# Stick-breaking attention: the two heads of a pair in one step, logits on the halves of the array's rows, values on the halves of its columns with the operands exchanged

## The chip, the cores and the metric

One core of a Trainium2 chip runs the whole program; seven others lie idle. The metric is the device time of one execution in microseconds (us). TensorE (PE in the profile) multiplies matrices, VectorE (DVE) and ScalarE (ACT) work element by element, GpSimd (POOL) starts the gathers, SyncE (SP) starts the other transfers.

## The reference, cut to what matters

One decoder layer on 1024 tokens of width 1024: a mixer of three branches (stick-breaking attention, sparse attention, HGRN2 recurrence), and then PEER, a layer of 16384 small experts of which each token takes 128. The change touches the first branch alone, which has 8 heads of 64:

```python
for i in range(T // Q_BLOCK):                      # blocks of 128 queries
    q0 = i * Q_BLOCK
    kl = q0 + Q_BLOCK
    z = jnp.einsum("bhtd,bhsd->bhts", q[:, :, q0:kl], k[:, :, :kl]).astype(jnp.float32) * scale
    before = jnp.arange(kl)[None, :] < (q0 + jnp.arange(Q_BLOCK))[:, None]
    log_1m = jnp.where(before, jax.nn.log_sigmoid(-z), 0.0)
    after = lax.cumsum(log_1m, axis=3, reverse=True) - log_1m
    a = jnp.where(before, jnp.exp(jax.nn.log_sigmoid(z) + after), 0.0)
    outs.append(jnp.einsum("bhts,bhsd->bhtd", a.astype(v.dtype), v[:, :, :kl]))
```

So block i of queries needs i + 1 blocks of 128 keys: 36 blocks for a head, 288 for the eight.

## The kernel before

**Stages.** The tokens go through the mixer in four parts of 256. A part has four rounds; each round takes one head of HGRN2 (`hg`), one group and token tile of the sparse attention (`ns`) and one pair of heads of the stick-breaking attention (`sb`). The experts of parts 1 and 2 are then computed for all tokens by TensorE ("dense": 128 blocks of 48 matmuls, L1353 on). Parts 0 and 3 have theirs fetched row by row: 1024 gathers of 512 KB (L1104, L1114), each followed by one VectorE instruction of 1024 columns (L1106, L1116). 420 of these rows are paced to go beside the mixer, the others beside the dense experts. The mixer ends, and the dense products of the second kind begin, at about 2071 us.

**Items and pieces.** The branches' chains are lists of items of up to four stages. In step t of the order of emission the first stage of item t goes out, then the second of t-1, the fourth of t-3, the third of t-2 (L1302). What stands on its own (projections, merges, norms, scores, routes, the spreading of the gates) is cut into pieces. Each step is filled with pieces up to an even load:

```python
RPE, RDVE, REND, PD = 3.5, 3.0, 5.0, 1.2           # L24: work of TensorE and VectorE that a step is filled up to
for p in todo:                                     # L1297: pieces whose latest step has come go first
    if p.before > t:
        break
    p.emit(t)
```

A piece has a latest step; where it is reached the piece goes out whatever the load is (here called forced). The rows are paced by step numbers too: none before step 135, then 420 in proportion to the steps' TensorE work (L26, L1075). A scheduler then orders each engine's queue from this; what it made can be read in the built program, engine by engine.

**The branch that is changed** (`sb_items`, L372). An item is one head, one tile of 128 queries and up to 512 keys. `logits` (L381): one fp32 matmul of 64 rows (the head's width) into a PSUM bank `z`, for the first keys the mask as a second matmul (L387), then Abs, Relu, Exp, Ln on ScalarE. `weights` (L394): a running sum on VectorE (L397), its last column kept for the next chunk, a subtraction that reads `z` again (L401) and frees it, an Exp. `turned` (L404): transposes by TensorE into a bank `tr`, a copy `aT` to SBUF. `values` (L411): for each block of 128 keys a matmul with `aT` (128 columns) as the stationary operand and 64 columns of `v` moving; the result has the queries on the partitions. At the end of a round `out` and `out2` (L426, L430) copy the result, transpose it back by TensorE and split it into two float16 parts.

There are two banks `z` (ZB, L30), three banks `tr`, one bank `ov` and eight buffers `at` (e, r and aT of this branch, and what others keep for a short time). The heads of a pair lie on partitions 0 to 63 and 64 to 127 of `q` and `k`.

An fp32 matmul that is no transpose stands in the trace as two weight loads and two matmuls.

Of the kernel before, what the change touches and what calls it, by code (L numbers as in the profile page):

```python
# [36 lines left out]
# operands of the large products are split into two float16 parts after scaling by these powers of two  # L37
# [4 lines left out]
# scales of the gates, of their spread over the experts, and of the activations in the dense experts  # L42
# [5 lines left out]
# block numbers in the stream of projection weights  # L48
# [5 lines left out]
class Part:  # L54
    """a run of tokens that goes through the mixer together"""
# [8 lines left out]
# the parts whose tokens go through all experts; the others' experts are gathered  # L64
# [5 lines left out]
def trunk(ctx: ExitStack, tc: tile.TileContext, a: dict, out: bass.AP):  # L70
# [13 lines left out]
    # what the mixer alone needs  # L84
# [44 lines left out]
    # strictly causal block in reversed key order: key 127 - x, allowed where 127 - x < p  # L129
# [3 lines left out]
    # causal block: key x allowed where p - x >= 0  # L133
# [3 lines left out]
    # for each length of segments: keys of a first half before queries of the second, the second halves' queries only  # L137
# [7 lines left out]
    # distances to the keys of the window and to the ends of the blocks, negative; far under where the key isn't seen  # L145
# [11 lines left out]
    # lower bounds: cumulative softmax over the layers less the first layer's share  # L157
# [12 lines left out]
    # the window's keys and values: this part's and the one's before  # L170
# [49 lines left out]
    def load_w(blk, name, pt, br=False):  # L220
        """a block of weights in two parts; split for the first part, kept in DRAM for the others"""
# [29 lines left out]
    def transposed(src, name, pre=False):  # L251
        """the 128-column blocks of src transposed, side by side in one bank"""
# [44 lines left out]
    # Work comes in two kinds. Pieces stand on their own (projections, norms, merges); items are steps of the  # L297
    # branches' chains, each cut into four stages so that several can be under way at once.
# [37 lines left out]
    def sb_pieces(p, pt, st):  # L336
# [3 lines left out]
        def keep(t, d):  # L340
            # the tokens of earlier parts come back from DRAM
# [10 lines left out]
        # keys and values in reversed token order  # L352
# [19 lines left out]
    def sb_items(p, pt, st):  # L372
# [3 lines left out]
        def chunk(tl, hh, c0, c1, W):  # L376
            r0, n, b = T - W, c1 - c0, hh * 64
            un = f"{nm}_{tl}_{hh}_{c0}"
            x = {}

            def logits():  # L381
                z = ps_z.tile([128, 512], F32, tag="z", name=f"z_{un}")
                x["e"] = e = W2(f"e_{un}")
                x["z"], x["ee"] = z[:, 0:n], e[:, 0:n]
                P.matmul(x["z"], st["q"][b:b + 64, tl * 128:(tl + 1) * 128], st["k"][b:b + 64, r0 + c0:r0 + c1], start=True, stop=(c0 > 0))
                if c0 == 0:
                    P.matmul(z[:, 0:128], identb, sbmask, start=False, stop=True)  # L387
                x["r"] = W2(f"r_{un}")[:, 0:n]
                S.activation(x["ee"], x["z"], AF.Abs)
                S.activation(x["r"], x["z"], AF.Relu)  # L390
                S.activation(x["ee"], x["ee"], AF.Exp, scale=-1.0)
                S.activation(x["ee"], x["ee"], AF.Ln, bias=1.0)

            def weights():  # L394
                ee = x["ee"]
                # sum of softplus from the last key down, the key itself included
                V.tensor_tensor_scan(ee, x["r"], ee, 0.0 if c0 == 0 else st["prev"], op0=ALU.add, op1=ALU.add)  # L397
                if c1 < W:
                    st["prev"] = SM(f"prev_{un}", [128, 1])
                    V.tensor_copy(st["prev"], x["e"][:, n - 1:n])  # L400
                V.tensor_tensor(ee, x["z"], ee, op=ALU.subtract)  # L401
                S.activation(ee, ee, AF.Exp)

            def turned():  # L404
                tr = ps_tr.tile([128, TH], F32, tag="tr", name=f"tra_{un}")
                for c in range(0, n, 128):
                    P.transpose(tr[:, c:c + 128], x["e"][:, c:c + 128], ident)
                x["aT"] = W2(f"aT_{un}")
                S.activation(x["aT"][:, 0:n], tr[:, 0:n], AF.Copy)

            def values():  # L411
                if tl == 0 and hh == 0 and c0 == 0:
                    st["ov"] = ps_ov.tile([128, 4, 128], F32, tag="ov", name=f"ov_{nm}")
                for c in range(0, n, 128):
                    vb = r0 + c0 + c
                    P.matmul(st["ov"][:, tl, b:b + 64], x["aT"][:, c:c + 128], st["v"][:, vb + b:vb + b + 64], start=(c0 + c == 0), stop=(c0 + c == W - 128))
# [3 lines left out]
        for tl in range(pt.nt):  # L420
            W = 128 * (pt.ti0 + tl + 1)
            for hh in range(2):
                for c0 in range(0, W, 512):
                    res.append(chunk(tl, hh, c0, min(W, c0 + 512), W))

        def out():  # L426
            st["o"] = W2(f"o_{nm}", (128, pt.n))
            S.activation(st["o"], st["ov"][:, 0:pt.nt].rearrange("p a b -> p (a b)"), AF.Copy)

        def out2():  # L430
            oh, ol = branch_out(pt, 0)
            tr = transposed(st["o"], f"o_{nm}")
            split(oh[:, p, :], ol[:, p, :], tr, SO[0])

        res.append([None, None, out, out2])
        return res

# [1 line left out]
    def nsa_kv_pieces(pt, st):  # L439
# [22 lines left out]
        # compression of keys and values: block c takes the pieces c and c + 1 of 16 tokens.  # L462
        # Two neighbouring positions lie one under the other on the partitions; columns: position pair, group, block
# [3 lines left out]
        def pieces(which):  # L467
# [13 lines left out]
            # the last piece is kept for the next part  # L481
# [48 lines left out]
    def nsa_items(g, tl, pt, st, kv):  # L530
# [9 lines left out]
        # compressed branch  # L540
        def c_logits():
# [6 lines left out]
            # a column of nothing before the first block  # L548
# [19 lines left out]
        def c_select():  # L568
            # importance of the blocks: the heads' weights of the five pieces that overlap; sure blocks at the top
# [7 lines left out]
            # the four best are struck out, by value and place  # L577
# [6 lines left out]
        def c_rows():  # L584
            # the block bias and the distance penalty as further rows of the queries
# [18 lines left out]
        # the selection is found and used while the window's heads go on  # L604
        res = [[c_logits, c_norm, c_turn, c_values], [None, c_select, None, None], None, [None, None, c_rows, None]]

        # window branch, then selected branch, one head at a time
        sums = {}

        def head(br, i):  # L610
# [9 lines left out]
            def logits():  # L620
# [3 lines left out]
                # logits, negative, and the least of them  # L624
# [77 lines left out]
    def hg_pieces(h, pt, st):  # L702
        """projections of a head: values token-major; gates raw"""
# [21 lines left out]
    def hg_items(h, pt, st):  # L725
# [770 lines left out]
```

## Time and profile before

| | |
|---|---|
| three runs | 3733.98, 3744.84, 3757.71 us; median 3744.84 |
| span of the profiled execution | 3722.6 us; its own time with what lies around the span is not on the page |
| busy share of the span | PE 88%, PEld 59%, DVE 82%, ACT 42%, POOL 34% |
| mean TensorE clock granted | 0.921 |
| bytes moved | 1055.48 MB, mean 284 GB/s |

The three runs lie within 0.6% of each other. A window's row names a stretch of the span in us, and the busy time of each engine in it; a timeline's row gives the start, the time from the first start to the last end, and how many equal instructions follow each other. Matmuls are pipelined, so that the time of one is longer than the interval from its start to the next one's.

### The profile page before, as it was taken

Reading aid. Unit: us, or ns where it says so; the run is one execution under the profiler, and the core shown is the slowest. Engines: PE = TensorE matmul, PEld = TensorE weight load, DVE = VectorE, ACT = ScalarE, POOL = GpSimd, SP = SyncE. Lnnn points to the kernel's source line nnn. Section 1 sums busy time; section 2 is a strip of 40 time slices with the busy share of each in tenths; the row PEclk is TensorE's granted clock in tenths of the full one; section 3 lists DMA queues with packets and bytes.
Section 4 is the critical chain, followed back from the end, with each engine's and each line's share of the span. In section 5 each row is a group of like instructions: output and inputs, shape, how many; then the busy total and the mean of one; then the engine's idle time right before and its main releaser. Section 6 shows DMA issues by size and latency. Waiting matters only on the chain. (4 is left out here: it accounts for less than half of the span.)

```text
span 3722.6 us, 57637 instructions
## 1 busy us (share of the span) xinstructions
PE 3285.9 (88%) x20660; PEld 2191.0 (59%) x20660; DVE 3035.8 (82%) x7067; ACT 1572.2 (42%) x3110; POOL 1275.4 (34%) x1167
## 2 busy tenths in 40 slices
PE   6999999999986999898878897859999999999993
PEld 5887777777875777786566453424444444444441
DVE  5665689788799888789988678988888887888886
ACT  4776456554444564554457223323232223223222
POOL 0000002343322432233222344144555554555554
PEclk9999999999995999898577999979999999999996
DMA  7964857889974878877465999579999999999987
GB/s 260 334 243 144 295 189 274 317 308 325 328 273 147 300 256 300 296 278 261 142 208 195 356 332 325 193 273 339 333 337 325 320 337 322 346 332 318 334 287 261
DMA packets 359916, 1055.48 MB, mean 284 GB/s; under 512 B 35814, under 2 KB 108330, under 8 KB 355532
## 3 DMA queue, kind: packets, MB, share of 16 engines
q0 software_dynamic: 147456, 536.94, 41.5%
q1 hardware_dynamic: 212172, 514.86, 38.7%
q8 instruction: 162, 2.65, 0.3%
q14 instruction: 126, 1.03, 0.1%
HBM read 943.66 MB, written 108.00 MB: 283 GB/s over the span
## 5 line engine op out<-in xcount | busy, mean ns | idle before, releaser
L1114 POOL DMA_INDIRECT v<-in_peer_v_dram,gidx x512 | 655.1, 1280 | 872.7 <-DVE gacc L1116 590.8
L1104 POOL DMA_INDIRECT u<-in_peer_u_dram,gidx x512 | 605.9, 1183 | 869.1 <-DVE u L1106 599.4
L242 PE MATMUL g<-h,us 128*128 128x512 f16 x3072 | 712.5, 390 | 109.0 <-DVE acc L1383 71.4
L1116 DVE SCALAR_TENSOR_TENSOR gacc<-v,act,gacc 128x1024 f32<-128x1024 f32 x512 | 654.6, 1278 | 112.2 <-DMA v<-in_peer_v_dram,gidx 104.8
L1106 DVE SCALAR_TENSOR_TENSOR u<-u,gh 128x1024 f32<-128x1024 f32 x512 | 618.1, 1219 | 124.6 <-DMA u<-in_peer_u_dram,gidx 123.2
L242 PEld LDWEIGHTS <-us 128*128 128x128 f16 x3072 | 306.1, 100 | 497.8 <-issue 115.4
L1375 PE MATMUL acc<-vs,ac 128*128 128x512 f16 x2304 | 536.3, 384 | 33.1 <-ACT ac L200 28.4
L1375 PEld LDWEIGHTS <-ac 128*128 128x128 f16 x3072 | 302.9, 99 | 414.2 <-ACT ac L200 30.9
L242 PE MATMUL pj_mg<-hT,w_mg 128*128 128x256 f16 x2304 | 279.1, 277 | 16.3 <-ACT mg L859 9.5
L242 PEld LDWEIGHTS <-w_mg 128*128 128x128 f16 x2304 | 229.5, 101 | 48.8 <-issue 20.7
L200 ACT ACTIVATE vs<-vraw 128x1024 f16<-128x1024 f32 x128 | 133.8, 1048 | 270.3 <-DMA vraw<-in_peer_v_dram 270.1
L200 ACT ACTIVATE ac<-ge 128x512 f16<-128x512 f32 x128 | 79.9, 626 | 365.8 <-DVE ge L1368 250.0
L1335 ACT ACTIVATE ge<-g 128x512 f32<-128x512 f32 x128 | 75.6, 590 | 362.7 <-PE g L242 362.6
L1375 PE MATMUL g<-vs,ac 128*128 128x512 f16 x768 | 179.5, 385 | 9.6 <-DVE ts L958 7.3
L201 DVE SCALAR_TENSOR_TENSOR vs<-vraw,vs 128x1024 f16<-128x1024 f32 x128 | 155.2, 1217 | 23.2 <-ACT vs L200 23.2
L1174 PE MATMUL gb<-hot 128*128 128x128 f16 x512 | 126.3, 295 | 44.6 <-ACT stage L1177 28.9
L1177 ACT ACTIVATE stage<-gb 128x512 f32<-128x512 f32 x128 | 131.9, 1070 | 79.0 <-DMA d_G<-stage 45.2
L200 ACT ACTIVATE us<-uraw 128x1024 f16<-128x1024 f32 x128 | 134.0, 1049 | 68.2 <-DMA uraw<-in_peer_uT_dram 52.6
L242 PE MATMUL pb<-o,w_b 128*128 128x256 f16 x1152 | 141.6, 279 | 19.4 <-DMA w_b<-dw 9.3
L201 DVE SCALAR_TENSOR_TENSOR us<-uraw,us 128x1024 f16<-128x1024 f32 x128 | 155.7, 1218 | 2.9 <-ACT us L200 2.7
L242 PE MATMUL pj_r_hg<-hT,w_r_hg 128*128 128x256 f16 x1152 | 138.2, 277 | 1.5 <-ACT iv_hg L715 0.7
L242 PEld LDWEIGHTS <-w_b 128*128 128x128 f16 x1152 | 113.8, 101 | 42.6 <-issue 14.5
(1133 smaller groups left out, 5944.0 us busy)
## 6 DMA issues: line engine op xcount, KB each, us to landing
uraw<-in_peer_uT_dram SPq DMA_DIRECT2D x128, 512.0 KB, 6.7
vraw<-in_peer_v_dram SPq DMA_DIRECT2D x128, 512.0 KB, 6.2
w_mg<-dw SPq DMA_DIRECT2D x72, 512.0 KB, 6.3
d_G<-stage SPq DMA_DIRECT2D x32, 1024.0 KB, 5.1
gt<-d_G SPq DMA_DIRECT2D x32, 1024.0 KB, 13.2
w_r_hg<-dw SPq DMA_DIRECT2D x36, 512.0 KB, 5.7
w_b<-dw SPq DMA_DIRECT2D x72, 256.0 KB, 5.9
wr_mg<-in_wblk_dram SPq DMA_DIRECT2D x24, 512.0 KB, 5.1
```

What stands on the lines that cost most here:

```text
L200: S.activation(hi, src, AF.Copy, scale=scale)
L201: V.scalar_tensor_tensor(lo, in0=src, scalar=scale, in1=hi, op0=ALU.mult, op1=ALU.subtract)
L242: P.matmul(ps, l[:, k, :], r[:, k, :], start=(i == 0), stop=(i == n - 1))
L1104: G.indirect_dma_start(out=ur, out_offset=None, in_=a["peer_u"], in_offset=bass.IndirectOffsetOnAxis(ap=idx[:, c:c + 1], axis=0))
L1106: V.scalar_tensor_tensor(ur, in0=ur, scalar=1.0, in1=h2, op0=ALU.mult, op1=ALU.mult, accum_out=hpre[:, c:c + 1])
L1114: G.indirect_dma_start(out=vr, out_offset=None, in_=a["peer_v"], in_offset=bass.IndirectOffsetOnAxis(ap=idx[:, c:c + 1], axis=0))
L1116: V.scalar_tensor_tensor(acc, in0=vr, scalar=act[:, c:c + 1], in1=acc, op0=ALU.mult, op1=ALU.add)
L1174: P.matmul(ps[:, n, :], hs[:, 0, :, n], hs[:, 2, :, n], start=True, stop=False)
L1177: S.activation(stage[0][:, :, m0:m0 + 4].rearrange("p i n -> p n i"), ps, AF.Copy, scale=SA / SGT)
L1335: S.activation(ge, ps, AF.Gelu, scale=1.0 / (SW * SH2))
L1375: P.matmul(ps, ac[:, x, t * 128:(t + 1) * 128], v[:, y, dh * 512:(dh + 1) * 512], start=start and n == 0, stop=stop and n == 2)
```

## The change

An item is now a pair of heads: `logits` issues the two matmuls one behind the other, the first head's on rows 0 to 63 of the array into one bank `z`, the second's on rows 64 to 127 into the other, and then each head's mask and ScalarE work. `weights` and `turned` do one head after the other. `values` has `v` (64 columns) as the stationary operand and `aT` (128 columns) moving; the two heads alternate, the first on columns 0 to 63 of the array, the second on columns 64 to 127. The result has the channels on the partitions already, so the copy, the transposes back and one stage of the last item go. The items of a round fall from 5 to 3 in parts 0 and 1, from 9 to 5 in parts 2 and 3; 456 items become 408. The constants (RPE, PACE0 and so on) stay. Elsewhere comments alone are gone, so that line numbers behind this place are higher by 3.

```diff
-        def chunk(tl, hh, c0, c1, W):
-            r0, n, b = T - W, c1 - c0, hh * 64
-            un = f"{nm}_{tl}_{hh}_{c0}"
-            x = {}
+        def chunk(tl, c0, c1, W):
+            r0, n = T - W, c1 - c0
+            un = f"{nm}_{tl}_{c0}"
+            heads = [{}, {}]
             def logits():
-                z = ps_z.tile([128, 512], F32, tag="z", name=f"z_{un}")
-                x["e"] = e = W2(f"e_{un}")
-                x["z"], x["ee"] = z[:, 0:n], e[:, 0:n]
-                P.matmul(x["z"], st["q"][b:b + 64, ...], st["k"][b:b + 64, ...], start=True, stop=(c0 > 0))
-                if c0 == 0:
-                    P.matmul(z[:, 0:128], identb, sbmask, start=False, stop=True)
-                x["r"] = W2(f"r_{un}")[:, 0:n]
-                ...
+                for hh, x in enumerate(heads):
+                    b = hh * 64
+                    x["zt"] = z = ps_z.tile([128, 512], F32, tag="z", name=f"z_{un}_{hh}")
+                    x["z"] = z[:, 0:n]
+                    P.matmul(x["z"], st["q"][b:b + 64, ...], st["k"][b:b + 64, ...], start=True, stop=(c0 > 0))
+                for hh, x in enumerate(heads):
+                    if c0 == 0:
+                        P.matmul(x["zt"][:, 0:128], identb, sbmask, start=False, stop=True)
+                    ...
             def weights():
-                ...
+                for hh, x in enumerate(heads):
+                    ...
             def turned():
-                ...
+                for hh, x in enumerate(heads):
+                    ...
             def values():
-                if tl == 0 and hh == 0 and c0 == 0:
-                    st["ov"] = ps_ov.tile([128, 4, 128], F32, tag="ov", name=f"ov_{nm}")
+                if tl == 0 and c0 == 0:
+                    st["ov"] = ps_ov.tile([128, TH], F32, tag="ov", name=f"ov_{nm}")
                 for c in range(0, n, 128):
                     vb = r0 + c0 + c
-                    P.matmul(st["ov"][:, tl, b:b + 64], x["aT"][:, c:c + 128], st["v"][:, vb + b:vb + b + 64], ...)
+                    for hh, x in enumerate(heads):
+                        b = hh * 64
+                        P.matmul(st["ov"][b:b + 64, tl * 128:(tl + 1) * 128], st["v"][:, vb + b:vb + b + 64], x["aT"][:, c:c + 128], ...)
         for tl in range(pt.nt):
             W = 128 * (pt.ti0 + tl + 1)
-            for hh in range(2):
-                for c0 in range(0, W, 512):
-                    res.append(chunk(tl, hh, c0, min(W, c0 + 512), W))
+            for c0 in range(0, W, 512):
+                res.append(chunk(tl, c0, min(W, c0 + 512), W))
         def out():
-            st["o"] = W2(f"o_{nm}", (128, pt.n))
-            S.activation(st["o"], st["ov"][:, 0:pt.nt].rearrange("p a b -> p (a b)"), AF.Copy)
-        def out2():
             oh, ol = branch_out(pt, 0)
-            tr = transposed(st["o"], f"o_{nm}")
-            split(oh[:, p, :], ol[:, p, :], tr, SO[0])
-        res.append([None, None, out, out2])
+            split(oh[:, p, :], ol[:, p, :], st["ov"][:, 0:pt.n], SO[0])
+        res.append([None, None, None, out])
```

More of the change, by code (lines that the diff above doesn't have):

```diff
@@ new lines, in logits @@
+                for hh, x in enumerate(heads):
+                    b = hh * 64
+                    x["zt"] = z = ps_z.tile([128, 512], F32, tag="z", name=f"z_{un}_{hh}")
+                    x["z"] = z[:, 0:n]
+                    P.matmul(x["z"], st["q"][b:b + 64, tl * 128:(tl + 1) * 128], st["k"][b:b + 64, r0 + c0:r0 + c1], start=True, stop=(c0 > 0))
+                for hh, x in enumerate(heads):
+                    if c0 == 0:
+                        P.matmul(x["zt"][:, 0:128], identb, sbmask, start=False, stop=True)
+                    x["e"] = e = W2(f"e_{un}_{hh}")
+                    x["ee"] = e[:, 0:n]
+                    x["r"] = W2(f"r_{un}_{hh}")[:, 0:n]
+                    S.activation(x["ee"], x["z"], AF.Abs)
+                    S.activation(x["r"], x["z"], AF.Relu)
+                    S.activation(x["ee"], x["ee"], AF.Exp, scale=-1.0)
+                    S.activation(x["ee"], x["ee"], AF.Ln, bias=1.0)
@@ new lines, in weights @@
+            def weights():
+                for hh, x in enumerate(heads):
+                    ee = x["ee"]
+                    V.tensor_tensor_scan(ee, x["r"], ee, 0.0 if c0 == 0 else st["prev", hh], op0=ALU.add, op1=ALU.add)
+                    if c1 < W:
+                        st["prev", hh] = SM(f"prev{hh}_{un}", [128, 1])
+                        V.tensor_copy(st["prev", hh], x["e"][:, n - 1:n])
+                    V.tensor_tensor(ee, x["z"], ee, op=ALU.subtract)
+                    S.activation(ee, ee, AF.Exp)
@@ L411, in values @@
+            def turned():
+                for hh, x in enumerate(heads):
+                    tr = ps_tr.tile([128, TH], F32, tag="tr", name=f"tra_{un}_{hh}")
+                    for c in range(0, n, 128):
+                        P.transpose(tr[:, c:c + 128], x["e"][:, c:c + 128], ident)
+                    x["aT"] = W2(f"aT_{un}_{hh}")
+                    S.activation(x["aT"][:, 0:n], tr[:, 0:n], AF.Copy)
             def values():
-                if tl == 0 and hh == 0 and c0 == 0:
-                    st["ov"] = ps_ov.tile([128, 4, 128], F32, tag="ov", name=f"ov_{nm}")
+                if tl == 0 and c0 == 0:
+                    st["ov"] = ps_ov.tile([128, TH], F32, tag="ov", name=f"ov_{nm}")
@@ L414, in values @@
                 for c in range(0, n, 128):
                     vb = r0 + c0 + c
-                    P.matmul(st["ov"][:, tl, b:b + 64], x["aT"][:, c:c + 128], st["v"][:, vb + b:vb + b + 64], start=(c0 + c == 0), stop=(c0 + c == W - 128))
+                    for hh, x in enumerate(heads):
+                        b = hh * 64
+                        P.matmul(st["ov"][b:b + 64, tl * 128:(tl + 1) * 128], st["v"][:, vb + b:vb + b + 64], x["aT"][:, c:c + 128], start=(c0 + c == 0), stop=(c0 + c == W - 128))
```

17 lines of the change are left out of this document (removed).

## The prediction

> **What bounds the kernel now.** I began with the page: the span, and the slices of the engines, of the clock and of the transfers.
>
> ```profile
> span 3722.6 us, 57637 instructions
> PE   6999999999986999898878897859999999999993
> DVE  5665689788799888789988678988888887888886
> PEclk9999999999995999898577999979999999999996
> DMA  7964857889974878877465999579999999999987
> ```
>
> TensorE is at nine tenths nearly everywhere, VectorE at eight, and where TensorE falls back its clock falls too. So I asked for the stages by windows: part 0, the rounds with rows beside them, one dip, the last rounds of the mixer, the tail of the last part, the dense experts.
>
> ```profile
> core 0: us, PE busy (x) PEld busy (x) DVE busy (x) ACT busy (x) POOL busy (x), PEclk, DMA share, GB/s
> 0.00:497.00 497.00, 440.79 (x3709) 376.71 (x3709) 295.73 (x741) 304.65 (x721) 5.97 (x69) 0.97 0.72 253
> 497.00:1100.00 603.00, 564.81 (x4467) 467.82 (x4467) 526.87 (x1714) 302.29 (x734) 196.07 (x208) 0.97 0.82 290
> 1100.00:1200.00 100.00, 68.25 (x300) 51.22 (x299) 95.58 (x355) 37.90 (x97) 25.39 (x32) 0.58 0.55 182
> 1200.00:1533.00 333.00, 303.48 (x2375) 254.30 (x2374) 284.22 (x644) 186.96 (x404) 111.89 (x103) 0.95 0.82 284
> 1533.00:2071.00 538.00, 466.96 (x3044) 366.35 (x3042) 464.53 (x1418) 283.41 (x552) 146.26 (x134) 0.80 0.66 231
> 2500.00:3655.00 1155.00, 1082.46 (x4876) 483.21 (x4877) 964.49 (x1277) 326.37 (x421) 609.90 (x466) 0.97 0.92 326
> ```
>
> The change lies in the first 2071 us. Up to 497 TensorE alone is the bound (441 of 497 us; VectorE 296). From 497 to 1533 the two are close, 937 and 907 of 1036 us. In the last 538 us VectorE has as much as TensorE (465 and 467), at a clock of 0.80. From 1100 to 1200 VectorE is full, TensorE waits and drops to a clock of 0.58. Behind 2500 the experts have a DMA share of 0.92 and none of the changed code. So TensorE work that is saved counts in about half of the mixer; elsewhere it becomes idle time.
>
> **What the branch costs TensorE.** Groups by line and form, then a timeline, because the interval from start to start is what an instruction takes from the engine:
>
> ```profile
> L416 PE MATMUL ov_sb<-v_sb,aT_sb 128*128 128x64 f32 x576 | 83.9, 287 | 9.9 <-ACT aT_sb L409 9.6
> L385 PE MATMUL z_sb<-k_sb,q_sb 64*128 64x512 f32 x96 | 62.0, 730 | 9.1 <-DVE e_sb L401 8.1 <-DVE nmx_ns3g1t0b1h L644 0.5 <-DVE nmx_ns2g1t0b1h L644 0.4
> ```
>
> ```profile
> 76.87 0.39 PE L830 MATMUL pS_hg<-iv_hg,kt_hg 128*128 128x128 f32 x2
> 77.18 2.05 PE L495 MATMUL pk_ns<-xp_ns,cw_ns 128*64 128x30 f32 x32
> 79.17 1.59 PE L242 MATMUL pj_ksel_ns<-hT,w_ksel_ns 128*128 128x256 f16 x13
> ...
> 152.65 0.33 PE L416 MATMUL ov_sb<-v_sb,aT_sb 128*128 128x64 f32 x2
> 152.81 0.60 PE L242 MATMUL pj_r_hg<-hT,w_r_hg 128*128 128x256 f16 x4
> 153.25 0.56 PE L416 MATMUL ov_sb<-v_sb,aT_sb 128*128 128x64 f32 x4
> 153.65 0.82 PE L242 MATMUL pj_r_hg<-hT,w_r_hg 128*128 128x256 f16 x6
> ...
> 1362.79 1.15 PE L242 MATMUL pj_ksel_ns<-hT,w_ksel_ns 128*128 128x256 f16 x9
> 1363.87 1.12 PE L495 MATMUL pk_ns<-xp_ns,cw_ns 128*64 128x32 f32 x16
> 1364.92 0.61 PE L242 MATMUL pj_ksel_ns<-hT,w_ksel_ns 128*128 128x256 f16 x4
> 1365.46 1.12 PE L385 MATMUL z_sb<-k_sb,q_sb 64*128 64x512 f32 x2
> 1366.52 0.23 PE L387 MATMUL z_sb<-sbmask,identb 128*128 128x128 bf16 x1
> 1366.58 0.82 PE L242 MATMUL pj_ksel_ns<-hT,w_ksel_ns 128*128 128x256 f16 x6
> 1367.24 0.60 PE L407 MATMUL tra_sb<-ident,e_sb 128*128 128x128 f32 x4
> ```
>
> The unit: six projections take 1366.58 to 1367.24, 0.11 us each.
>
> - Values now: four in 0.40 us, two in 0.16: 0.11 each, the first 0.05 less. They come in and go out without loss (four projections 152.81 to 153.25).
> - Rows: the logits use 64 rows of the array. Four projections should last 0.44 and take 0.54 (1364.92 to 1365.46): 0.10 to enter. Two matmuls of 512 fp32 columns (0.43 each: twice the time for a column that 256 columns in 0.11 show) take 1.06 instead of 0.86: 0.20 more, a weight load laid open and the way out. A visit to this form costs 0.30.
> - Columns: L495 uses 64 columns of the array with fp32, as the values will. Nine projections take 1.08 instead of 0.98: 0.10 to enter. 32 matmuls take 1.99, 16 take 1.05: 0.059 each, and about 0.11 once for a visit. With 128 moving columns instead of 32 the first weight load is covered by nothing (0.03 more): 0.24 a visit.
>
> **The change part by part.** How the instructions stand was read from the built program, each engine's queue.
>
> *Logits.* The source issues the two heads one behind the other, but an item now needs both banks `z`, and the bank of each head comes free by its own subtraction (L401). In the built queue only 8 of 48 pairs stand next to each other; between the others lie up to 146 instructions. The 8 save a visit each, 8 × 0.30 = 2.4 us. If the two also run at once, the second's columns are free: the 8 pairs have 3072 columns, at 2 × 0.43/512 us 5.2 us. No row shows two row halves at once; the bounds are 0 and 5.2, and I take half: −5.0 in all, between −2.4 and −7.6.
>
> *Values.* 576 matmuls in the trace, in 92 runs of the built queue: 576 × 0.112 − 92 × 0.05 = 59.9 us. Behind the change 576 with 128 moving columns at 0.109 (the projections' interval, the same 256 column times) = 62.8, in 83 runs, each now a visit to the column form: 83 × 0.24 = 19.9. Without overlap 82.7 us, 22.8 more than now. 205 of them stand directly behind one of the other head; each can hide one matmul of the two: 205 × 0.109 = 22.3, so 60.4 with full overlap, 0.5 more than now. What exchanging the operands can bring is eaten by the visits. Half: +11.7, between +0.5 and +22.8.
>
> The Trainium skill (TensorE: Matmul & The Clock Gate, Part 3) says that weight loads overlap running matmuls only where the row groups differ. By it each of the 576 column loads would lie open, some 0.05 × 576 = 29 us more; L495, whose loads share their rows, doesn't show it beyond the first.
>
> *Out.* Two transposes a round and a copy go:
>
> ```profile
> L259 PE MATMUL tr_o_sb<-ident,o_sb x32: 270/273/477, 161.1 to 2042.1; 128*128 128x128 f32 x32
> L428 ACT ACTIVATE o_sb<-ov_sb x16: 365/383/420, 159.1 to 2041.3; 128x256 f32<-128x256 f32 x16
> ```
>
> 32 × 0.109 = −3.5 us of TensorE. The copies, 16 × 0.383 = 6.1 us of ScalarE, lie beside TensorE's work (in the row 1200:1533 ScalarE is busy 187 of 333 us, TensorE 303): 0, at most −6.1.
>
> *VectorE, transfers.* Scans and subtractions stay in number and size; SyncE's queue loses one entry in 1053, GpSimd's none. Nothing.
>
> *TensorE's sum:* −5.0 + 11.7 − 3.5 = +3.2 us, from −10.6 (everything overlaps) to +16.9 (nothing). It counts where TensorE is the longer engine; about half of the branch's work lies in such stages, so +1.6.
>
> *The waits.*
>
> ```profile
> PE trr L1145 <- DVE fb_rt L1041: 17.3, 1, 17.3
> PE z_sb L385 <- DVE e_sb L401: 12.2, 11, 1.8
> PE ov_sb L416 <- ACT aT_sb L409: 9.6, 8, 4.0
> ```
>
> A pair takes both banks, so its logits wait for the pair before; its values wait for two `aT`. Queued behind them are the projections (L242), for which the PSUM copies on ScalarE wait. Now these two waits are 21.8 us in all; the scheduler sets other work between, as before. I take 0; the bounds are −21.8 (gone) and +21.8 (doubled).
>
> *Order.* The items fall from 456 to 408, and each step still draws 3.5 us of TensorE and 3.0 of VectorE work in pieces. Counted in the order of emission, 606 pieces fill steps and 75 are forced by their latest step; behind the change 498 and 183. So the filling comes later, in lumps, and the rows a little later (404 stand before the mixer's end, then 397). Where does that move work? For each third of a round I summed both queues with the durations of the trace and took the longer engine. The sum is 1979 us before and 1978 after (the trace has 2012 us for it, 59.3 to 2071.3: 33 lost to waits). On the way it runs ahead by 43 us, up to the second round of the last part, and gives 42 back in the last three rounds, where VectorE gets what was put off. So −1. For the lumps I add 5; a lump's cost is bounded below.
>
> *In all:* 1.6 − 1 + 5 = +6 on the span of 3722.6, so 3729. The median of the runs is 22 above the span, the fastest 11; I forecast 3744.84 + 6 = **3750 us**, no change that can be told. A measurement of this kernel tells about 1%, 37 us.
>
> **The rivals.**
>
> *The halves overlap fully.* TensorE gets 10.6 us back, waits stay: 3734 to 3740. For it: 205 of the values do alternate. Against: no row shows overlap, and half of the mixer isn't TensorE's. The Trainium skill (the same page, Part 3) has matmuls on different tiles start some 4 ns apart and three column tiles 2.38 times as fast; that is this rival, and no run here shows it yet. 0.13.
>
> *Faster: the work put off finds room.* The 43 us that the middle rounds lose aren't given back, because VectorE idles 538 − 465 = 73 us in the last window. 3745 − 43 = 3702. For it: that idle time. Against: it lies between short waits, and what is put off is a chain. 0.15.
>
> *Slower: the lumps.* A forced chain of routes, scores and merges fills VectorE while TensorE waits, as in 1100:1200, where the transposes of a route (trr, above) wait 17.3 us for VectorE and the clock halves. If the 33 us lost grow with the forced pieces, 33 × (183 − 75)/75 = 47 more: 3792. It decides from about 37 us. For it: the constants are in steps, and the steps are fewer; the third round of parts 2 and 3 gets 22 and 25 forced pieces at its start. Against: the scheduler spreads lumps. 0.30.
>
> *The change doesn't do what it says:* no half ever overlaps, +16.9 at TensorE: 3752 to 3762, in the forecast's band.
>
> **How the numbers follow.** The forecast with its own band (no overlap to half) has 0.42; 3725 to 3775 is its range. Faster by over 1% is 0.15, slower by over 1% 0.30, within 1% 0.13 + 0.42 = 0.55. The range goes to both other cases with the two waits' bound on the slow side: 3700 to 3805.
>
> **What would show it.** Right: the values' group keeps about 576 matmuls, entering them costs 0.10 us, only few logits pairs start together; the mixer ends between 2050 and 2095. A values run of eight (16 matmuls) that takes about 1.0 us shows overlap, about 2.0 none. The slower case shows dips of TensorE and its clock with a full VectorE in the third rounds of parts 2 and 3; the faster one a VectorE over 0.92 busy in the last 500 us of the mixer. Wrong altogether: time that moves behind 2500 us, where nothing changed.

## The result and the profile after

The changed kernel takes 3779.06 us (median of 5 runs, 3773.25 to 3784.71). Against the kernel before, run beside it, the ratio is 1.0091, with a 95% interval of 1.0065 to 1.0117: slower by 0.9%, some 34 us. Forecast were 3750 us, with a range of 3700 to 3805. The profiled execution has a span of 3771.3 us, 6 under its median once the 2 us around the span are counted. The slices of the changed kernel's page, as they were shown of before:

```profile
span 3771.3 us, 57638 instructions
PE   6999999999986989898777897759999899998994
DVE  5665689888699888879987778988888887877887
PEclk9999999999986999997667998889999999999997
DMA  7963857889865878857465999589999999998988
```

The picture is that of before: the same dips, the last rounds of the mixer at a lower clock, and transfers at nine tenths behind it. The stages by windows (us, then busy time and number of instructions of PE, PEld, DVE, ACT, POOL; granted clock, DMA share, GB/s); the mixer now ends at 2087:

```profile
core 0: us, PE busy (x) PEld busy (x) DVE busy (x) ACT busy (x) POOL busy (x), PEclk, DMA share, GB/s
0.00:497.00 497.00, 441.47 (x3687) 374.26 (x3688) 293.45 (x739) 303.25 (x716) 5.96 (x69) 0.96 0.72 252
497.00:1100.00 603.00, 562.29 (x4506) 459.32 (x4504) 515.19 (x1743) 305.95 (x741) 180.21 (x193) 0.97 0.79 279
1100.00:1200.00 100.00, 56.73 (x259) 41.30 (x257) 94.05 (x310) 36.38 (x93) 31.62 (x38) 0.61 0.63 212
1200.00:1533.00 333.00, 305.48 (x2380) 248.56 (x2380) 282.45 (x639) 195.40 (x422) 101.63 (x102) 0.92 0.79 280
1533.00:2087.00 554.00, 460.80 (x3034) 346.96 (x3031) 471.07 (x1431) 287.06 (x538) 141.19 (x136) 0.79 0.65 227
2500.00:3655.00 1155.00, 1047.20 (x4681) 465.52 (x4682) 942.67 (x1274) 320.07 (x410) 590.37 (x455) 0.95 0.92 320
```

Two things are to be seen. In the last rounds TensorE has somewhat less to do than before (461 against 467 us) and they take 16 us longer. And the last row, in which no line was changed, does less in the same 1155 us: 4681 matmuls instead of 4876, 320 GB/s instead of 326, at the same DMA share of 0.92. The transfers are as busy and move less. Part of that is the later start, since more blocks with left-over rows fall into the window. The whole stretch is measured by `ge`, the product of activations and gates, which VectorE takes twice in each of the 128 blocks; the first one marks the mixer's end. Its line before and after (the two times behind the durations are the first and the last start):

```profile
L1368 DVE TENSOR_TENSOR ge<-ge,gt x256: 400/419/496, 2071.3 to 3658.6; 128x256 f32<-128x256 f32 x128
```

```profile
L1371 DVE TENSOR_TENSOR ge<-ge,gt x256: 397/419/490, 2087.5 to 3712.5; 128x256 f32<-128x256 f32 x128
```

From the first ge to the last the changed kernel takes 1625 us, the profile before 1587: 38 of the 49 us between the two profiles lie there.

What the branch costs TensorE, groups by line and form, then two stretches of the timeline:

```profile
L425 PE MATMUL ov_sb<-aT_sb,v_sb 128*64 128x128 f32 x576 | 65.5, 310 | 17.1 <-ACT aT_sb L416 14.9 <-DVE ob_ns1g1t0b1h L685 2.1
L387 PE MATMUL z_sb<-k_sb,q_sb 64*128 64x512 f32 x96 | 61.8, 776 | 12.0 <-DVE e_sb L407 8.9 <-DVE nmx_ns3g1t0b1h L647 1.4 <-DVE u_n L216 1.3
```

```profile
152.94 0.60 PE L242 MATMUL pj_q_sb<-hT,w_q_sb 128*128 128x256 f16 x4
153.47 0.66 PE L425 MATMUL ov_sb<-aT_sb,v_sb 128*64 128x128 f32 x8
154.06 0.72 PE L242 MATMUL pj_q_sb<-hT,w_q_sb 128*128 128x256 f16 x5
...
1019.24 0.49 PE L242 MATMUL pj_pq<-h,w_pq 128*128 128x256 f16 x3
1019.66 1.13 PE L387 MATMUL z_sb<-k_sb,q_sb 64*128 64x512 f32 x4
```

The halves run at once, fully. The eight values at 153.47 start 7 ns apart in pairs; the first pair takes 0.16 us, each further one 0.11, and the way in and the way out cost 0.10 each beyond the projections' interval. So the values' group has 65.5 us of busy time instead of 83.9. The four records at 1019.66 are the logits of two heads with 512 columns each; they take the 1.13 us that one head took before (1.12 at 1365.46). In the whole trace 8 pairs of logits meet so, and 202 pairs of the values' 576 records (a matmul leaves two).

And the waits of the mixer, the three of TensorE that were shown of before:

```profile
PE trr L1148 <- DVE fb_rt L1044: 27.0, 1, 27.0
PE z_sb L387 <- DVE e_sb L407: 16.6, 9, 3.3
PE ov_sb L425 <- ACT aT_sb L416: 14.9, 9, 4.7
```

The whole mixer, before and after:

```profile
0.00:2071.30 2071.30, 1844.29 (x13888) 1516.40 (x13888) 1666.95 (x4868) 1115.20 (x2506) 485.57 (x545) 0.91 0.74 259
```

```profile
0.00:2087.50 2087.50, 1826.77 (x13856) 1470.40 (x13856) 1656.21 (x4861) 1128.03 (x2507) 460.61 (x538) 0.90 0.73 256
```

TensorE is busy 17 us less and idle 34 us more (261 instead of 227 us).

### The profile page after: what moved, and what is told of

Same layout as the page of the kernel before. It is cut to its first block, busy times and chain, and to the rows that moved or that the text cites. A ratio compares the mean times of both kernels' runs of the same rounds, so it can differ in the third digit from the quotient of the medians.

```text
span 3771.3 us, 57638 instructions
## 1 busy us (share of the span) xinstructions
PE 3273.0 (87%) x20628; PEld 2146.4 (57%) x20628; DVE 3034.4 (80%) x7067; ACT 1586.2 (42%) x3111; POOL 1259.4 (33%) x1167
## 4 chain that ended last, share of the span: by engine, by line
PE 25%; DVE 20%; issue 19%; DMA 19%; POOL 9%; ACT 8%; SPq 0%; POOLq 0%; DVEq 0%; ACTq 0%
DMA v<-in_peer_v_dram,gidx 11%; POOL u L1107 6%; PE pj_mg L242 4%; DMA u<-in_peer_u_dram,gidx 3%; DVE gacc L1119 3%; POOL v L1117 3%; DVE u L1109 3%; PE pj_r_hg L242 2%; PE pj_wo L242 2%; PE pb L242 1%; PE z_sb L387 1%; DMA d_G<-stage 1%; DVE ts L965 1%; PE gb L1177 1%; DVE ts L961 1%
## 5 line engine op out<-in xcount | busy, mean ns | idle before, releaser
L1117 POOL DMA_INDIRECT v<-in_peer_v_dram,gidx x512 | 637.6, 1245 | 897.6 <-DVE gacc L1119 633.3
L242 PE MATMUL g<-h,us 128*128 128x512 f16 x3072 | 721.4, 394 | 142.0 <-DVE acc L1386 90.1
L1371 DVE TENSOR_TENSOR ge<-ge,gt 128x256 f32<-128x256 f32 x256 | 99.9, 427 | 45.6 <-DMA gt<-d_G 35.6
```

The source lines that it names most:

```text
L242: P.matmul(ps, l[:, k, :], r[:, k, :], start=(i == 0), stop=(i == n - 1))
L1117: G.indirect_dma_start(out=vr, out_offset=None, in_=a["peer_v"], in_offset=bass.IndirectOffsetOnAxis(ap=idx[:, c:c + 1], axis=0))
L1371: V.tensor_tensor(gv, gv, gt[:, :, i % 8, :], op=ALU.mult)
```

## The experiments

Three theories stood at the start. *Steps:* there are 408 steps instead of 456, so the filling comes late and in lumps. *Pairs:* a step of two heads waits for two banks `z` and two `aT`. *Values:* the exchanged values are dearer in themselves. A fourth, *addresses*, came out of the traces and the built programs.

**The kernel before, profiled again.**

> The kernel before, once more, for a second profile. Ratio 1.000 (0.997 to 1.003) by every theory. What it tells apart is the later part of the loss: behind the mixer (first ge to last ge) the kernel before took 1588 us and the changed one 1625. If this 37 us is the state of the transfers in one execution, the second profile lies anywhere between 1588 and 1625; if the change causes it (seven rows fewer done before the mixer's end, then 0.3 us more a block), it stays within 1580 to 1597, and the mixer ends at 2066 to 2077 us.

3743.07 us, ratio 1.0006 (0.9988 to 1.0024). The span is 3743.8, so this profile lies near the median, where the first one lay 22 us under it. The mixer ends at 2084.5 instead of 2071.3, and from the first to the last ge it takes 1595 us (before 1587). Of the changed kernel's 1625, 30 remain that no execution of the kernel before shows.

**An empty step behind each pair.**

```
                 res.append(chunk(tl, c0, min(W, c0 + 512), W))
+                res.append([None, None, None, None])
```

> The changed kernel with an empty step behind each step of a pair, so that there are 456 steps again and 603 pieces fill steps, 78 are forced (before 606 and 75, changed 498 and 183). Theory 1 (fewer steps: the filling comes late and in lumps): ratio 0.995 to 1.000, the 10 us that the overlapping halves save at TensorE left over, mixer end 2060 to 2075. Theory 2 (a pair's waits for both banks z and both aT): the steps change nothing, ratio 1.007 to 1.012. Theory 3 (the exchanged values themselves are dearer): the same as theory 2 here, told apart by the next two kernels.

3820.81 us, ratio 1.0219 (1.0200 to 1.0237): a miss for all three. The theory of the steps expected the loss gone, and it doubled, though the forced pieces were 78 again. The way there tells what the steps do. A round begins here with its first decay product `att`, and rounds are counted from 0. From the start of round 1 of the last part to the mixer's end the kernel before takes 534 us in both profiles, the changed one 582, this one 527. The end of the mixer did get its time back; but the rounds up to there took 1601 us instead of 1506 (before 1537 and 1550). The number of steps moves work from one place to another; it doesn't make the sum smaller. (Its buffers lie as the changed kernel's do, so what the addresses cost, below, is part of its loss.)

**Two old steps in one.**

```
-            for hh in range(2):
-                for c0 in range(0, W, 512):
-                    res.append(chunk(tl, hh, c0, min(W, c0 + 512), W))
+            one = [chunk(tl, hh, c0, ...) for hh in range(2) for c0 in range(0, W, 512)]
+            for A, B in zip(one[0::2], one[1::2]):
+                res.append([lambda f=f, g=g: (f(), g()) for f, g in zip(A, B)])
```

> The kernel before with two of its steps of the stick-breaking branch in one (408 steps, 507 pieces fill steps, 174 are forced), the values and the transposed output as before, the operands not exchanged. Theory 1 (steps): slower as the changed kernel, 1.008 to 1.015, since TensorE's saving of 10 us is missing. Theory 2 (waits of two heads in one step): also 1.006 to 1.012. Theory 3 (exchanged values): 0.998 to 1.002.

3791.32 us, ratio 1.0130 (1.0110 to 1.0149). So steps of two chunks alone, with the old values, cost 1.3%; no exchanged values are needed for a loss. The mixer ends at 2127, 43 us behind the second profile of before. For the long tiles, though, the two chunks here are of one head, the second going on from the first's sum, and not of two heads: the 43 us can't be put on pairs of heads.

**The exchanged values alone.**

```
-                    P.matmul(st["ov"][:, tl, b:b + 64], x["aT"][:, c:c + 128], st["v"][:, vb + b:vb + b + 64], ...)
+                    P.matmul(st["ov"][b:b + 64, tl * 128:(tl + 1) * 128], st["v"][:, vb + b:vb + b + 64], x["aT"][:, c:c + 128], ...)
```

> The kernel before with the values' operands exchanged on column halves and the output taken without transposes, but one head a step (456 steps, 598 pieces fill steps, 83 are forced). The halves then meet less often. Theory 1 (steps): 0.997 to 1.003. Theory 2 (waits of pairs): the same. Theory 3 (exchanged values dearer, 83 or more visits at 0.2 us and no overlap): 1.005 to 1.010.

3753.09 us, ratio 1.0028 (1.0013 to 1.0043). Between the theories: a loss of 10 us that is real but small. Here only 9 records of the values start together with one of the other half. What the values occupy of TensorE is counted from each start to the start of its next matmul, idle time left out, and with what the instruction in front of a visit takes beyond its usual interval. They occupy 88 us here, 73 in the kernel before and 68 in the changed one. So the visits to the column form do cost 15 us when hardly anything overlaps, and the pairs more than pay for them.

**The changed kernel again, and a third bank `z`.** The view of VectorE's waits had one that had grown more than any: the scans of the branch, for ScalarE's logarithm. The kernel before (second profile), the changed one, the changed one with three banks; total, times, longest:

```profile
DVE e_sb L397 <- ACT e_sb L392: 30.5, 23, 3.8
```

```profile
DVE e_sb L403 <- ACT e_sb L397: 71.1, 34, 8.7
```

```profile
DVE e_sb L403 <- ACT e_sb L397: 44.3, 26, 5.2
```

A pair holds both banks, so the logits of the next can't be computed ahead of its subtractions. With a third bank they can; the bank is taken from the transposes, and the kernel before with the same banks is the measure.

```
-RB, WB, AT, ZB, TB = 5, 4, 8, 2, 3
+RB, WB, AT, ZB, TB = 5, 4, 8, 3, 2
```

> The changed kernel once more, for a second profile. Ratio 1.006 to 1.012. From the first to the last ge the kernel before took 1588 and 1596 us in two profiles, the changed one 1625 in one; 3.5 rows that are left over at the mixer's end are worth 3.5 x 1.05 MB / 0.32 MB per us = 11 us of that. If the remaining 18 us are the state of the transfers, this profile has 1595 to 1612; if they belong to the change, 1618 to 1632. The mixer's end lies at 2080 to 2095 in both cases.

> The changed kernel with three banks z and two for transposes instead of two and three. A pair takes both banks z, so no logits can be computed ahead of the subtractions of the pair before; behind the change VectorE's scans waited 71 us for ScalarE's logarithm (before 30 us), in the pairs with old values 72. Theory B (banks): the third bank lets the first head of the next pair go ahead, the scans' wait falls under 55 us, and the distance to the kernel before with the same banks shrinks from +0.9% to between 0 and +0.5%. Theory S (steps, 183 forced pieces, as many as with two banks): the distance stays +0.7% to +1.2%.

> The kernel before with three banks z and two for transposes: the measure for the run above. Either theory: 0.995 to 1.010, as the missing bank for transposes costs or the third z pays; the scans' wait for ScalarE stays at 25 to 40 us.

The repeat: 1.0095 (1.0070 to 1.0119); mixer's end 2097, then 1636 us to the last ge. So the long dense stretch is no matter of one execution; it belongs to the changed kernel. With three banks: changed 1.0173 (1.0146 to 1.0199), before 1.0060 (1.0037 to 1.0082), a distance of 1.0173/1.0060 = 1.011. The scans' wait fell from 71 to 44 us as the theory of the banks has it (39 in the kernel before with the same banks), and the distance did not shrink. Some 0.5% of it are the addresses, below, which the changed kernel has and the other has not; the 0.6% left are no less than the 0.43% that the change costs with two banks. That wait isn't what sets the time, and the theory falls.

**Both heads in one bank.** Chunks of 256 keys; the queries of each head padded with zeros to 128 rows; both heads in one bank; one instruction for two heads on ScalarE, and on VectorE in all but the scan:

```
+                z = ps_z.tile([128, 2, 256], F32, tag="z", name=f"z_{un}")
+                for hh in range(2):
+                    P.matmul(z[:, hh, 0:n], st["q"][:, hh, ...], st["k"][:, r0 + c0:r0 + c1], ...)
...
+                    st["prev"] = SM(f"prev_{un}", [128, 2])
...
-            for c0 in range(0, W, 512):
+            for c0 in range(0, W, 256):
```

> The changed kernel with pieces of 256 keys instead of 512 for both heads of a pair in one bank z, one tile e, one bank of transposes; the queries of each head are padded with zeros to all 128 rows of the array, so the logits are no longer in the row form. Two pairs can now be under way in the two banks z; ScalarE's and VectorE's instructions for two heads are one (the scan apart). 440 steps, 561 pieces fill steps, 120 are forced. Theory B (banks): the scans' wait for ScalarE falls to 40 us or less, ratio 0.988 to 0.999. Theory S (steps): part of the lumps stay, 1.002 to 1.008.

3731.03 us, ratio 0.9968 (0.9952 to 0.9985): faster than both kernels. Wait and ratio are as the theory of the banks had them, but so much changes at once here that this doesn't show the banks to be the reason. The scans' wait fell to 36.7 us; the mixer ends at 2076, no earlier than the 2071 and 2084 of the kernel before, although TensorE is busy 1791 instead of 1855 us up to there. What stands out is the stretch behind it: 1582 us from the first to the last ge, against 1625 and 1636 of the changed kernel.

**The addresses.** Until then the dense stretch had been compared as a whole, and the changed kernel leaves 3.5 gathered rows more to it (a row is two gathers). From block 32 on nearly the same rows are left in all kernels (455 to 457 gathers). There eight kernels gave 1083 to 1096 or 1101 to 1116 us, and the line between them was no queue but a list of addresses. The source names the two tiles for the last column of the sums `prev0` and `prev1`; a pool keeps buffers for each name, so the pool of small tiles grew by 64 bytes, and everything behind it moved by as much: the buffers of the gathered rows, the weights and the activations begin at 320 instead of 256 modulo 512 bytes. In the diff this is the line

```
-                    st["prev"] = SM(f"prev_{un}", [128, 1])
+                        st["prev", hh] = SM(f"prev{hh}_{un}", [128, 1])
```

Three kernels test it. The first has one tile of two columns in the changed kernel, with the order of every queue unchanged:

```
-                        st["prev", hh] = SM(f"prev{hh}_{un}", [128, 1])
-                        V.tensor_copy(st["prev", hh], x["e"][:, n - 1:n])
+                        if hh == 0:
+                            new = SM(f"prev_{un}", [128, 2])
+                        V.tensor_copy(new[:, hh:hh + 1], x["e"][:, n - 1:n])
+                        if hh == 1:
+                            st["prev"] = new
```

The second and third put an unused tile of 64 or 128 bytes into the kernel before:

```
+    G.memset(SM("pad_0", [128, 16], bufs=1), 0.0)
```

> The changed kernel with the last column of both heads' sums in one small tile prev of two columns instead of two tiles prev0 and prev1. Every queue is that of the changed kernel; but the pool of small tiles is 64 bytes shorter, as in the kernel before, so that all buffers behind it (gathered rows, weights, activations) begin again at 256 instead of 320 modulo 512 bytes. Theory A (addresses): from block 32 of the dense experts on, where the same rows go with each block, the kernels with 256 took 1083 to 1096 us and those with 320 took 1101 to 1116; this one takes 1083 to 1098, the dense stretch 1588 to 1610 instead of 1625 and 1636 (11 us stay for 3.5 rows left over), and the ratio falls from 1.009 to 0.999 to 1.004. Theory R (order of rows and blocks): 1105 to 1118, dense stretch 1620 to 1638, ratio 1.007 to 1.012.

> The kernel before with an unused small tile of 64 bytes (and one memset of it at the start): the queues of the kernel before, the addresses of the changed one. Theory A (addresses): dense stretch 1605 to 1625 instead of 1587 and 1595, from block 32 on 1101 to 1116, ratio 1.004 to 1.010. Theory R: as the kernel before, ratio 0.998 to 1.002.

> The kernel before with an unused small tile of 128 bytes: the buffers behind the small tiles begin at 384 modulo 512 bytes. If what counts is a multiple of 128 bytes, ratio 0.998 to 1.002; if a multiple of 256, as with 64 bytes: 1.004 to 1.010. By theory R 0.998 to 1.002 too.

The changed kernel with the old addresses: 3756.32 us, ratio 1.0043 (1.0022 to 1.0065), at the upper end of what theory A had; its dense stretch is 1605 us. The kernel before with 64 bytes more: 1.0052 (1.0030 to 1.0074); with 128 bytes more: 1.0052 (1.0029 to 1.0074). The windows from block 32 to the last block: the kernel before (second profile), the kernel before with 64 bytes more, the changed kernel, the changed kernel with the old addresses.

```profile
2583.98:3679.79 1095.81, 1012.78 (x4557) 452.03 (x4556) 897.41 (x1169) 300.40 (x388) 578.42 (x438) 0.96 0.91 321
```

```profile
2595.88:3708.80 1112.92, 1019.50 (x4561) 453.43 (x4560) 897.98 (x1169) 300.59 (x388) 572.13 (x439) 0.96 0.92 316
```

```profile
2602.72:3712.45 1109.73, 1019.64 (x4560) 453.47 (x4558) 898.75 (x1167) 300.82 (x388) 566.81 (x438) 0.96 0.92 318
```

```profile
2601.81:3692.22 1090.41, 1013.82 (x4564) 452.49 (x4563) 896.95 (x1168) 300.56 (x388) 568.93 (x438) 0.97 0.92 324
```

The same matmuls, VectorE busy for 897 to 899 us in all four, DMA share 0.91 or 0.92; only the rate differs, and it follows the addresses and not the queues. In the stretch the transfers moved, by the view of the DMA queues of the kernel before and of the same with 64 bytes more:

```profile
DMA packets 135999, 352.27 MB, mean 321 GB/s; under 512 B 10392, under 2 KB 55817, under 8 KB 135937
```

```profile
DMA packets 135804, 352.21 MB, mean 316 GB/s; under 512 B 10377, under 2 KB 55611, under 8 KB 135742
```

352.3 MB and 352.2 MB, as much, in 17 us more. The packets show it one by one: in this stretch a packet of 512 bytes takes 27.4 to 27.6 ns on the mean in the eight profiles with 256 or 0 modulo 512, and 29.6 to 29.9 ns in the six others; one of 4096 bytes takes 181.7 to 183.2 and 183.0 to 185.0. VectorE's and ScalarE's instructions, which read and write the moved buffers too, are as long in the four rows above (897 to 899 and 300 to 301 us), so it is the transfers that suffer. The theory of the addresses holds, in both directions; that of the order doesn't explain this part. A multiple of 128 bytes isn't enough: the kernel with 384 modulo 512 took 1107 us. Over all fourteen profiles the eight whose buffers begin at a multiple of 256 bytes have 1083 to 1096 us, the six others 1101 to 1116.

The Trainium skill (DMA: Bandwidth & Descriptors, How a descriptor splits into AXI transactions) says that a transfer's descriptor is cut into pieces of 256 bytes, and that one which doesn't begin at a multiple of 256 starts at the boundary below and fetches bytes that aren't used. The traces agree with it as to the boundary: 256 and 0 modulo 512 are fast, 320 and 384 slow. They say nothing of the fetching: the buffers that moved are those in SBUF, which nearly all transfers of this stretch fill. An estimate by that page: a row of 4096 bytes needs 17 pieces instead of 16 at either offset, and 130 beats instead of 128 at 64 bytes, 132 at 128. The measured 1.7% (six profiles at 1108 us on the mean, eight at 1090) is near that of the beats at 64 bytes, 1.6%; but 128 bytes cost no more than 64 (1107 and 1113), so the beats don't explain both. No run here shows the pieces themselves.

**One bank, at 0 modulo 512.** A constant of 256 bytes moved behind the other buffers:

```
-    identb = cst.tile([128, 128], BF16, name="identb")
+    identb = per.tile([128, 128], BF16, name="identb")
```

> The kernel with both heads in one bank, and a constant of 256 bytes (identb) moved behind the other buffers: the queues of that kernel, but the buffers that the transfers fill begin at 0 instead of 256 modulo 512 bytes. It was 0.9968 of the kernel before. If multiples of 512 bytes carry the transfers better still, as 256 did against 320 and 384 (1090 against 1108 us from block 32 on): 0.990 to 0.995, 1065 to 1085 us. If 256 is enough: 0.995 to 0.999, 1083 to 1096 us.

3726.91 us, ratio 0.9949 (0.9932 to 0.9966), from block 32 on 1086 us. That is within what 256 modulo 512 gave (1091 us, 0.9968 with an interval that overlaps), so 512 wins nothing that can be told. It has the lowest ratio of this study, 0.5% under the kernel before.

## Why the prediction was right, and where it was wrong

The time lies in the range and, barely, in the band of 1% that had the largest chance, but 4 us outside the forecast's own 3725 to 3775, and the interval of 1.0065 to 1.0117 leaves no room for "no change that can be told". That the range holds it is in good part luck: half of the loss has a cause that the prediction put at nothing. With the experiments the loss, 0.91% to 0.95%, falls into two halves. The addresses are worth 0.5%, some 19 us (64 bytes more in the kernel before: 1.0052; taken out of the changed one: from 1.0091 and 1.0095 to 1.0043). The change itself is worth 0.43%, 16 us: the mixer ends about 10 us later (2071, 2084, 2085 and 2080 in four profiles with the queues of before, 2087, 2097 and 2087 with those of the change; the groups come within 2 us of each other, so the 10 us are rough), blocks 16 to 32 take 12 us longer with the rows left over (228 to 240 us), and the end behind the last ge is 4 to 5 us shorter.

- *The stages* are as read: the same up to 497 us (TensorE 441 us both times), TensorE and VectorE close together behind that.
- *Logits, −5.0.* Only 8 pairs meet, as the built queue said, and they overlap fully, which is what the bound of −7.6 assumes. By the count of start to start the logits occupy TensorE for 101 to 102 us in four profiles with the queues of before and for 97 to 101 in three with those of the change: some −3. Why it isn't more stays open.
- *Values, +11.7.* Wrong was the half of the overlap that was taken. It is full in 202 pairs (205 were counted), and the values went from 73 to 68 us (66 in two further profiles of the changed queues): −5 or more, under the lower bound of +0.5. The visit was sized rightly, 0.24 against the 0.10, 0.05 and 0.10 measured, though its 0.03 had no row behind it. Too small were the 59.9 us for the values before: they had each interval at 0.112, and some 55 of the intervals in the trace are 0.21, as fits a granted clock of 0.80 in the last rounds. The kernel without pairs shows the other end, +15, where +22.8 was worked out. The Trainium skill (TensorE: Matmul & The Clock Gate, Part 3) was quoted with two rules: that weight loads overlap only where the row groups differ doesn't hold here (0.11 us a pair, both loads included); that matmuls on different tiles start some 4 ns apart and run together does, at 7 ns.
- *TensorE's sum, +3.2.* Its sign was wrong: −3 − 5 − 3.5 (the transposes of the output are gone) is −11 or −12, near the bound of −10.6 with everything overlapping. TensorE's busy time up to the mixer's end, in which the pipelined ends count too, is 1844 to 1858 us in four profiles with the queues of before and 1827 to 1832 in three with those of the change: some 20 us less. They brought nothing: the mixer became longer.
- *The waits, 0 between −21.8 and +21.8.* TensorE's two waits rose from 21.8 to 31.5 us, inside the bounds. The wait that changed most wasn't on the list, which had TensorE's alone: VectorE's scans, from 30 to 71 us. It was the obvious suspect, and the third bank showed that less of it makes the kernel no faster. What was missed is TensorE's idle time as a whole: 227 to 231 us up to the mixer's end in the four profiles, 257 to 265 in the three, 30 more against 20 saved. Some 25 of the 30 lie in the last three rounds, spread over many waits; the largest rise among them is for VectorE at the spreading of the gates, from 12.7 to 21.4 us.
- *Order, −1, and lumps, +5.* The shape came as summed: ahead by 32 us at round 1 of the last part against the first profile (45 against the second; 43 was the sum), and given back, 48 us in the last three rounds (42). The lumps were mis-sized: the mixer ends some 10 us later, where 1.6 − 1 + 5 were summed, although TensorE's term turned out a saving. And the rows, 404 and 397 gathers before its end as counted, were given no price and cost 12 us. The dip of 1100 to 1200 grew as the slower rival has it, TensorE 57 instead of 68 us busy, the wait of the route's transposes 27 instead of 17 us. Its other sign, dips in the third rounds of parts 2 and 3, came weakly: TensorE's idle time in that of part 2, in which this dip lies, rose from 37 or 38 us to between 41 and 46, in that of part 3 from between 26 and 30 to 36 or 37.
- *"VectorE, transfers … Nothing."* This step failed. No transfer was added, but the buffers in SBUF that they fill were moved by 64 bytes, which cost some 19 us. "Wrong altogether: time that moves behind 2500 us" was the sign, and it came. Nothing in the profile of before speaks of it; the list of addresses of the changed kernel does, and it was there to be read beside the queues.

Of the rivals, full overlap (0.13) was right in its mechanism and wrong in its time: 3734 to 3740 were named, since it left the waits and the order as they were. The slower one was right in its direction, and its waits of TensorE for VectorE did grow; the 16 us that the change itself costs are a third of its 47.

What stays open is the cause in the mixer itself. That its last rounds have more waits is seen, why the order brings them was not shown. The empty steps show that the step count moves work, the third bank that the scans' wait doesn't set the time; why steps of two chunks with the old values cost 43 us there, and why the empty steps slow the earlier rounds by some 50, wasn't settled.

## What to carry to other kernels

Behind a change compare the addresses of the buffers as well as the queues: a new name in a pool can move everything behind it, and where transfers set the pace a start off a multiple of 256 bytes cost 0.5% here, through a tile of 4 bytes. When time is lost in a stretch whose code didn't change, look for what that stretch shares with the change, and test it with a kernel whose queues are untouched. TensorE's time that is saved in a mixer with several limits is no gain until the end of the stage shows it: here 20 us were saved and 10 lost.

## What the runs showed of the hardware that was not expected

- Matmuls in fp32 on the two column halves, and on the two row halves, start 7 ns apart and run at once: 0.11 us for a pair of records with 128 moving columns, 1.13 us for the four records of two matmuls with 512.
- Going into the column form costs 0.10 us, going out 0.10, and the first pair of a visit 0.05 more; the further weight loads lie beside the running matmuls although they use the same rows.
- Transfers of the same 352 MB take 1.7% longer where their buffers begin at 320 or 384 instead of 256 modulo 512 bytes, at the same DMA share: the share of busy time doesn't show it, the rate and the time of a packet do (512 bytes: 27.5 to 29.7 ns).
